# Token mixing with two shifted projections: a load that is issued later, and a crossbar transpose in two parts

## The chip, the cores and the metric

The kernel runs on one core of a Trainium2 chip. A core has TensorE (PE in the profile) for matmuls, VectorE (DVE), ScalarE (ACT) and GpSimd (POOL) for elementwise work, and SyncE (SP), which here only issues transfers. Sixteen DMA engines move data between the chip's memory and the core's SBUF. Each engine takes its instructions in program order; across engines the order is set by semaphores. The metric is the device time of the whole kernel in microseconds.

## The reference, cut to what matters

```python
batch, seq_len, d_model = (16, 2048, 256)
x_prev[:, 1:, :] = x[:, :-1, :]                       # the row before; zeros for the first
xv = x * time_mix_v + x_prev * (1 - time_mix_v)
xr = x * time_mix_r + x_prev * (1 - time_mix_r)
v = xv @ value_weight
r = xr @ receptance_weight
out = (sigmoid(r) * v) @ output_weight
# xk and k are computed in the reference too, and nothing uses them
```

The output is fp32, 16 x 2048 x 256. The kernel folds `time_mix` into the weights, so that what it has to form per element is `x + c * x_prev` with `c = 1/time_mix - 1`, once for r and once for v.

## The kernel before: the parts that the change touches

The 32768 rows are worked off in 64 units of 512 rows, four to a batch. For unit g, TensorE computes r(g) and v(g) into PSUM (psum_r, psum_v, one buffer each), ScalarE takes the sigmoid of r(g), VectorE multiplies it with v(g) into z(g), TensorE multiplies z with the output weight into psum_o (one buffer), and ScalarE evicts psum_o into o_sb, from which SyncE stores.

The matmuls need x with channels on the partitions. For batches 0 to 10 TensorE transposes blocks of 128x128 and ScalarE copies them to `xt`; for the last five batches the crossbar of the DMA does it, by transposes that SyncE issues. Batches 0 and 1 are loaded by units, and batch 2 onward by whole batches. Within a batch `xt` has 16 slots of 128 rows, and one slot 0 ahead of them: as rows are dealt to partitions, `x_prev` of slot j is slot j - 1, and slot 0 is slot 16 moved by one row. That copy is made by ScalarE for the last five batches.

```python
    def load(b):                                  # GpSimd issues: fp32 in memory, bf16 in SBUF
        if b not in x_bf:
            x_bf[b] = xpool.tile([P, J, D], BF16, name="x_bf")
        if b < BYUNIT:                            # batches 0 and 1: four loads, one for each unit
            for e in range(UB):
                nc.gpsimd.dma_start(...)          # cut
            return
        if b < B - 1:
            run = 8192 if b < LONG else 16384
            return nc.gpsimd.dma_start(out=x_bf[b], in_=rows(b), max_dma_last_dim=run)
        return [...]                              # the last batch in two halves (cut)
    ...
    for e in (2, 3):
        nc.gpsimd.dma_start(out=x_first[:, e - 2], in_=unit_rows(x, 0, e)[:, 0])
    nc.gpsimd.dma_start(out=wo_bf, in_=output_weight.rearrange("(ko p) n -> p ko n", p=P))
    load(1)
    load(2)
    ...
    def by_dma(b, lo, hi, after=None):            # slots lo to hi of batch b through the crossbar
        op = nc.sync.dma_start_transpose(
            out=xt[b][:, 1 + lo : 1 + hi].rearrange("p j k c -> p (j k) c"),
            in_=x_bf[b][:, lo:hi].rearrange("p j d -> p (j d)"),
        )
        if after is not None:                     # not beside a load
            tc.add_manual_dep(op.ins, after.ins.name, SYNC, reason="not beside a load")
```

`x + c * x_prev` is built in two steps: a scaled copy of the shifted slots (`mix = c * xt`, by VectorE in L263, by GpSimd in L273, by ScalarE in L520), and an add of the unshifted slots by VectorE (L285). The loop over the units, cut to what matters here:

```python
    for g in range(NU - 1):
        ...                                       # r(g) on TensorE, sigmoid on ScalarE
        advance(...)                              # TensorE transposes for later units
        for b in range(B - 5, B):
            if g == max(UB * (b - 2) - 1, CROSS + (b > B - 5)):
                new_xt(b)
                if b == B - 5:                    # batch 11
                    for pair in kept.pop(g):
                        store(nc.sync, *pair, after=half_load)
                    by_dma(b, 0, J, last_load)
                else:
                    by_dma(b, 0, J)
                ...
            if g == UB * (b - 1) + 1:             # slot 0 out of the last slot (L554)
                nc.scalar.copy(out=xt[b][:, 0, :, 1:P], in_=xt[b][:, J, :, 0 : P - 1])
        if LATE_O < g < NU - 2:
            output(g - 2, z_prev2)                # TensorE: o(g-2); ScalarE: eviction (L351)
        ...
        if g == 1:
            scale_act(pieces(2)[1], (1,))
        ...                                       # scaled copies and adds on VectorE, v(g), z(g)
        for p in pooled[g]:
            wrap_slots(p, after=last)
            scale_pool(p, last)                   # GpSimd: the scaled copy L273
        for p in held[g]:
            add(p)
        ...
        if g == 1:
            advance(4)
```

Of the kernel before, what the change touches and what calls it, by code (L numbers as in the profile page):

```python
# [15 lines left out]
def kernel(  # L16
# [30 lines left out]
    J = S // P  # L47
    UJ = 4
# [47 lines left out]
    def rows(b):  # L96
        return x[b].rearrange("(p j) d -> p j d", p=P)

    def unit_rows(t, b, e, n=1):

        return t[b, e * TU : (e + n) * TU, :].rearrange("(e p j) d -> p e j d", p=P, j=UJ)

    def load(b):
        if b not in x_bf:
            x_bf[b] = xpool.tile([P, J, D], BF16, name="x_bf")
        if b < BYUNIT:
            for e in range(UB):
                nc.gpsimd.dma_start(
                    out=x_bf[b][:, e * UJ : (e + 1) * UJ, :], in_=unit_rows(x, b, e)[:, 0]
# [5 lines that stand above are left out]
        return [  # L115
            nc.gpsimd.dma_start(out=x_bf[b][:, j : j + J // 2], in_=rows(b)[:, j : j + J // 2])
            for j in (0, J // 2)
        ]
# [30 lines left out]
        nc.gpsimd.dma_start(out=x_first[:, e - 2], in_=unit_rows(x, 0, e)[:, 0])  # L149
    nc.gpsimd.dma_start(out=wo_bf, in_=output_weight.rearrange("(ko p) n -> p ko n", p=P))  # L150
    load(1)
    load(2)

    def warm_up(n):
        ps = ps_t_pool.tile([P, P], FP32, name="ps_t")
# [34 lines left out]
    def by_dma(b, lo, hi, after=None):  # L190
# [5 lines that stand above are left out]
        if after is not None:  # L196
            tc.add_manual_dep(op.ins, after.ins.name, SYNC, reason="not beside a load")
# [51 lines left out]
    def slots(piece, off=0):  # L249

        b, _, lo, hi = piece
        j = lo // P + (lo // TU if b < BYUNIT else 0) + off
        return slice(j, j + (hi - lo) // P)

    def mixed(piece):
        b, m, lo, hi = piece
        j = lo // P % (2 * UJ)
        return mix[(b * S + lo) // (2 * TU)][:, m, j : j + (hi - lo) // P]
# [42 lines left out]
    def project_unmixed(ps, mo):  # L301


        parts = [(w_prev[:, ko], ko, 0) for ko in range(KO)]
        parts += [(w_bf[:, 0, ko], ko, 1) for ko in range(KO)]
        for n, (w, ko, lo) in enumerate(parts):
            nc.tensor.matmul(
                out=ps[:, mo, :],
                lhsT=w[:, mo * P : (mo + 1) * P],
                rhs=xt[0][:, lo : lo + UJ, ko],  # L310
                start=(n == 0),
                stop=(n == len(parts) - 1),
            )
# [92 lines left out]
    def tile_for(b):  # L406

        if b not in mix:
            mix[b] = mixpool.tile([P, 2, 2 * UJ, KO, P], BF16, name="mix")

    def pieces(g):

        b, e = divmod(g, UB)
        tile_for(g // 2)
        return [(b, m, e * TU, (e + 1) * TU) for m in range(2)]

    def wrap_slots(piece, one=None, after=None):


        b, _, lo, _ = piece  # L420
        by_unit = b < BYUNIT
        key = (b, lo // TU if by_unit else UB - 1)
        if key not in late_copies:
            return
        kos = slice(0, KO) if one is None else slice(one, one + 1)
        if one in (None, KO - 1):
            late_copies.remove(key)
        j = slots(piece).start if by_unit else 0
        n = UJ if by_unit else J
        if by_unit and j > 0:  # L430
            engine = nc.vector if key == (0, 1) else nc.gpsimd
            engine.tensor_copy(out=xt[b][:, j, kos, 0:1], in_=xt[b][:, j - 1, kos, P - 1 : P])
        op = (nc.vector if after is None else nc.gpsimd).tensor_copy(  # L433
            out=xt[b][:, j, kos, 1:P], in_=xt[b][:, j + n, kos, 0 : P - 1]
        )
        if after is not None:
            tc.add_manual_dep(op.ins, after.ins.name, SYNC, reason="one at a time")
# [4 lines left out]
    def advance(limit):  # L442
        nonlocal tnext, half_load, last_load
        while tnext <= min(limit, NU - 1):
            b, e = divmod(tnext, UB)
            if b == 1 and e > 0:
                load(b + e + 1)
            elif b > 1 and e == 0 and b + 5 < B:
                if b == 2:
                    load(6)  # L450
                last_load = load(b + 5)
                if b + 5 == B - 1:
                    half_load, last_load = last_load
            if tnext < NU - BYDMA:
                transposes(tnext)
            tnext += 1
# [60 lines left out]
    def scale_act(piece, kos):  # L517
        b, m, _, _ = piece
        for ko in kos:
            nc.scalar.activation(  # L520
                out=mixed(piece)[:, :, ko],
                in_=xt[b][:, slots(piece), ko],
                func=ACT.Copy,
                scale=c_sb[:, m, ko : ko + 1],
            )

    z_prev2 = z_prev = None
    for g in range(NU - 1):
        ps_r = ps_r_pool.tile([P, KO, TU], FP32, name="psum_r")
        if g == 0:  # L530
            project_unmixed(ps_r, 0)
            advance(1)
            project_unmixed(ps_r, 1)
            wrap_slots(pieces(1)[0])
            scale(pieces(1)[0])
            last = add(pieces(1)[0])
        else:
            project(ps_r, g, 0)
        s_sb = zpool.tile([P, KO, TU], BF16, name="s_sb")
        nc.scalar.activation(out=s_sb, in_=ps_r, func=ACT.Sigmoid)  # L540
        advance(START_T[g] if g < len(START_T) else g + LOOK - (g == CROSS - 1))
# [3 lines that stand above are left out]
                if b == B - 5:  # L545
                    for pair in kept.pop(g):
                        store(nc.sync, *pair, after=half_load)
                    by_dma(b, 0, J, last_load)
                else:
                    by_dma(b, 0, J)  # L550
                for pair in kept.pop(g, []):
                    store(nc.sync, *pair)
            if g == UB * (b - 1) + 1:
                nc.scalar.copy(out=xt[b][:, 0, :, 1:P], in_=xt[b][:, J, :, 0 : P - 1])  # L554
        if LATE_O < g < NU - 2:
            output(g - 2, z_prev2)
        for p in products.get(g + 1, []):
            if g >= FREE and p[0][1] == 1:
                scale_act(p[0], (0,))
        for p in [q for q, _ in products[g]] + pooled[g]:  # L560
            last_unit_of = p[3] // TU - 1
            need = last_unit_of if p[0] < BYUNIT else min(last_unit_of + 1, UB - 1)
            assert UB * p[0] + need < tnext, (g, p, tnext)
            if g > AHEAD or p not in pooled[g]:
                wrap_slots(p)
        if g == 1:
            scale_act(pieces(2)[1], (1,))
        for p, kos in products[g]:
            if not (g - 1 >= FREE and p[1] == 1):
                scale(p, kos)  # L570
        for p in sums[g]:
            last = add(p)
        for p in pooled[g]:
            if p[0] >= BYUNIT:
                wrap_slots(p)
        ps_v = ps_v_pool.tile([P, KO, TU], FP32, name="psum_v")
        project(ps_v, g, 1)
        if g == 0:
            scale_act(pieces(1)[1], (0,))
            advance(2)  # L580
        z_sb = zpool.tile([P, KO, TU], BF16, name="z_sb")
        n = TU // 2 if g == NU - 2 else TU
        for c in range(0, TU, n):
            nc.vector.tensor_tensor(  # L584
                out=z_sb[:, :, c : c + n],
                in0=s_sb[:, :, c : c + n],
                in1=ps_v[:, :, c : c + n],
                op=ALU.mult,
            )
        for p in pooled[g]:  # L590
            wrap_slots(p, after=last)
            scale_pool(p, last)
        for p in held[g]:
            add(p)
        if z_prev is not None and not LATE_O <= g < NU - 3:
            output(g - 1, z_prev)
        if g == AHEAD - 2:
            scale_act(pieces(AHEAD)[0], (1,))
        if g == 1:
            advance(4)  # L600
        z_prev2, z_prev = z_prev, z_sb
# [31 lines left out]
```

## Time and profile before

The time before is 202.42 us, the median of three runs (202.08 to 202.89). The profiled execution spans 201.2 us.

| Part of the profile | What it says |
|---|---|
| idle time of TensorE | 201.2 - 195.1 = 6.1 us |
| TensorE, one matmul group of r, v or o | 0.86 to 0.87 us from one to the next |
| VectorE z (L584), 128x1024 | 1200 ns |
| VectorE add (L285), 128x1024 | 707 ns on average |
| GpSimd product (L273), 128x1024 | 1112 ns on average |
| ScalarE eviction (L351) | 1023 ns |
| mean use of the chip's memory | 337 GB/s over the span |
| crossbar transposes, issue to landing | 7.3 to 12.6 us |

The profile gives, for each group of instructions, the source line, the engine, what is written from what, and the idle time of the engine just ahead of it with the work that ended it. "PEld" is TensorE's loading of weights, which lies beside its matmuls. "SPq" and "POOLq" are the issuing queues of SyncE and GpSimd; the window of an issue is not the time of the transfer. A wait for several things is put down to the one that came last. The line numbers are those of the kernel before; in the changed kernel those between the removed line and the loop are one lower.

### The profile page before, as it was taken

The page shows a single profiled execution, that of the slowest core. Times are in us where ns is not written, and L with a number is a line of the kernel's source. Part 1 is how long each engine was busy: PE and PEld are TensorE (multiplying, and loading weights), DVE is VectorE, ACT ScalarE, POOL GpSimd, SP SyncE. Part 2 cuts the span into 40 slices and gives each one's busy share as a digit, 9 for nine tenths or more (in the row PEclk, how much of TensorE's full clock was granted, in tenths as well). Part 3 has the DMA queues.
Part 4 walks back from the last instruction along what each step waited for, and adds up shares of the span by engine and source line. Part 5 has one row for each costly group of instructions (what it writes and reads, how often), then busy time and mean ns, then how long its engine had stood idle before and what let it go on. Part 6 is the DMA issues. An engine that isn't in the chain of part 4 may idle for free.

```text
span 201.2 us, 3884 instructions
## 1 busy us (share of the span) xinstructions
PE 195.1 (97%) x1419; PEld 125.3 (62%) x1419; DVE 186.1 (93%) x292; ACT 181.0 (90%) x204; POOL 84.1 (42%) x115
## 2 busy tenths in 40 slices
PE   8989999999999999999999999998999999999992
PEld 6656676666666666666666666654656566555671
DVE  0899999999999999999999999999999999999982
ACT  3699899999999999999999999898999999999982
POOL 1766562452542543434452543443344444444200
PEclk9999999999999999999999999999999999999999
DMA  5899999999999999999999999899999999999675
GB/s 171 216 170 216 220 279 274 278 280 275 291 312 299 285 275 287 290 279 283 292 277 301 309 397 302 288 192 205 289 255 407 352 207 262 412 419 408 257 311 210
DMA packets 32410, 57.00 MB, mean 283 GB/s; under 512 B 21764, under 2 KB 23048, under 8 KB 28424
## 3 DMA queue, kind: packets, MB, share of 16 engines
q1 hardware_dynamic: 28176, 40.24, 58.8%
q0 software_dynamic: 4064, 16.39, 40.5%
q8 instruction: 11, 0.18, 0.3%
q10 hardware_dynamic: 152, 0.13, 0.2%
q14 instruction: 7, 0.06, 0.1%
HBM read 34.34 MB, written 33.55 MB: 337 GB/s over the span
## 4 chain that ended last, share of the span: by engine, by line
PE 80%; DMA 9%; DVE 4%; issue 2%; POOL 1%; ACT 1%; SPq 0%; DVEq 0%
PE psum_v L293 24%; PE psum_o L317 23%; PE psum_r L293 23%; PE ps_t L211 8%; DMA xt<-x_bf 4%; DMA x_bf<-in_x_dram 3%; DMA w_f<-n_receptance_weight_dram 2%; DVE mix L285 2%; DVE z_sb L584 2%; PE ps_t L317 1%; DVE mix L263 1%; POOL x_first L149 1%; ACT o_sb L351 1%; PE ps_t L293 0%; SPq L130 0%
## 5 line engine op out<-in xcount | busy, mean ns | idle before, releaser
L273 POOL TENSOR_SCALAR mix<-xt,c_sb 128x1024 bf16<-128x1024 bf16 (+1 forms) x55 | 61.2, 1112 | 93.6 <-DVE mix L285 84.3
L285 DVE TENSOR_TENSOR mix<-mix,xt 128x1024 bf16<-128x1024 bf16 x112 | 78.1, 707 | 1.9 <-DVE mix L263 0.5
L584 DVE TENSOR_TENSOR z_sb<-s_sb,psum_v 128x1024 bf16<-128x1024 bf16 (+1 forms) x64 | 76.7, 1200 | 3.3 <-PE psum_v L293 1.8
L293 PEld LDWEIGHTS <-w_bf 128*128 128x128 bf16 x516 | 48.7, 98 | 38.5 <-DVE mix L285 0.7
L540 ACT ACTIVATE s_sb<-psum_r 128x1024 bf16<-128x1024 f32 x63 | 65.3, 1036 | 3.3 <-PE psum_r L293 2.7
L351 ACT COPY o_sb<-psum_o 128x1024 f32<-128x1024 f32 x60 | 61.4, 1023 | 7.1 <-PE psum_o L317 7.0
L293 PE MATMUL psum_v<-mix,w_bf 128*128 128x512 bf16 (+1 forms) x256 | 65.3, 377 | 0.5 <-DVE mix L285 0.3
L293 PE MATMUL psum_r<-mix,w_bf 128*128 128x512 bf16 (+1 forms) x252 | 64.2, 377 | 0.1
L317 PE MATMUL psum_o<-wo_bf,z_sb 128*128 128x256 bf16 x486 | 63.2, 272 | 0.8 <-ACT o_sb L351 0.8
L317 PEld LDWEIGHTS <-z_sb 128*128 128x128 bf16 x512 | 49.8, 98 | 21.3 <-issue 2.2
L228 ACT COPY xt<-ps_t 128x1024 bf16<-128x1024 bf16 x36 | 37.0, 1041 | 0.0
L211 PEld LDWEIGHTS <-x_bf 128*128 128x128 bf16 x320 | 20.9, 98 | 8.9 <-DMA x_bf<-in_x_dram 0.7
L211 PE MATMUL ps_t<-ident,x_bf 128*128 128x128 bf16 x320 | 23.9, 219 | 0.2 <-DMA x_bf<-in_x_dram 0.2
L263 DVE TENSOR_SCALAR mix<-xt,c_sb 128x1024 bf16<-128x1024 bf16 (+1 forms) x49 | 22.0, 458 | 0.0
L520 ACT ACTIVATE mix<-xt,c_sb 128x1024 bf16<-128x1024 bf16 x12 | 13.9, 1157 | 0.0
L285 DVE TENSOR_TENSOR mix<-mix,xt_first 128x1024 bf16<-128x1024 bf16 x15 | 10.5, 709 | 0.3 <-ACT xt_first L228 0.3
L114 POOL DMA_DIRECT2D x_bf<-in_x_dram x13 | 8.6, 659 | 0.0
L263 DVE TENSOR_SCALAR mix<-xt_first,c_sb 128x512 bf16<-128x512 bf16 x21 | 6.2, 347 | 0.4 <-ACT xt_first L221 0.3
L228 ACT COPY xt_first<-ps_t 128x1024 bf16<-128x1024 bf16 x6 | 6.1, 1019 | 0.0
L157 PE MATMUL ps_t<-zeros 128*128 128x128 bf16 x30 | 3.6, 313 | 1.0 <-DVE zeros L90 1.0
L273 POOL TENSOR_SCALAR mix<-xt_first,c_sb 128x512 bf16<-128x512 bf16 x6 | 4.2, 694 | 0.5
L433 POOL COPY xt_first<-xt_first 128x254 bf16<-128x254 bf16 x5 | 2.0, 395 | 5.4 <-DVE mix L285 3.6
(70 smaller groups left out, 52.0 us busy)
## 6 DMA issues: line engine op xcount, KB each, us to landing
out_dram<-o_sb SPq DMA_DIRECT2D x28, 1024.0 KB, 14.9
x_bf<-in_x_dram POOLq DMA_DIRECT2D x13, 1024.0 KB, 24.8
out_dram<-o_sb SPq DMA_DIRECT2D x4, 512.0 KB, 2.8
out_dram<-o_sb SPq DMA_DIRECT2D x6, 256.0 KB, 2.5
o_sb<-in_x_dram SPq DMA_DIRECT2D x4, 256.0 KB, 4.0
x_bf<-in_x_dram POOLq DMA_DIRECT2D x4, 256.0 KB, 7.5
x_bf<-in_x_dram POOLq DMA_DIRECT2D x2, 512.0 KB, 11.5
x_first<-in_x_dram POOLq DMA_DIRECT2D x2, 256.0 KB, 4.1
```

Source lines behind the costliest of these rows:

```text
L114: return nc.gpsimd.dma_start(out=x_bf[b], in_=rows(b), max_dma_last_dim=run)
L211: nc.tensor.transpose(out=ps[:, jj], in_=src[:, jj, ko * P : (ko + 1) * P], identity=idn)
L228: nc.scalar.copy(out=xt[b][:, j0 : j0 + UJ], in_=ps)
L263: nc.vector.tensor_scalar(out=mixed(piece)[:, :, ko], in0=xt[b][:, slots(piece), ko], scalar1=c_sb[:, m, ko : ko + 1], scalar2=None, op0=A ...
L273: op = nc.gpsimd.tensor_scalar(out=mixed(piece)[:, :, 1], in0=xt[b][:, slots(piece), 1], scalar1=c_sb[:, m, 1:2], scalar2=1.0, op0=ALU.mul ...
L285: return nc.vector.tensor_tensor(out=mixed(piece), in0=mixed(piece), in1=xt[b][:, slots(piece, 1)], op=ALU.add)
L293: nc.tensor.matmul(out=ps[:, mo, :], lhsT=w_bf[:, m, ko, mo * P : (mo + 1) * P], rhs=mixed((b, m, e * TU + lo, e * TU + hi))[:, :, ko], st ...
L317: nc.tensor.matmul(out=ps[:, slot, :], lhsT=z[:, ko, jj * P : (jj + 1) * P], rhs=wo_bf[:, ko, :], start=(ko == 0), stop=(ko == KO - 1),)
L351: nc.scalar.copy(out=o_sb[b][:, j0 : j0 + UJ, :], in_=ps)
L520: nc.scalar.activation(out=mixed(piece)[:, :, ko], in_=xt[b][:, slots(piece), ko], func=ACT.Copy, scale=c_sb[:, m, ko : ko + 1],)
L540: nc.scalar.activation(out=s_sb, in_=ps_r, func=ACT.Sigmoid)
L584: nc.vector.tensor_tensor(out=z_sb[:, :, c : c + n], in0=s_sb[:, :, c : c + n], in1=ps_v[:, :, c : c + n], op=ALU.mult,)
```

## The change

Two things are moved, and the computation stays what it was.

```diff
     nc.gpsimd.dma_start(out=wo_bf, in_=output_weight.rearrange("(ko p) n -> p ko n", p=P))
     load(1)
-    load(2)
@@ in the loop over the units
                 if b == B - 5:
                     for pair in kept.pop(g):
                         store(nc.sync, *pair, after=half_load)
-                    by_dma(b, 0, J, last_load)
+                    by_dma(b, J - UJ, J, last_load)
+                    by_dma(b, 0, J - UJ, last_load)
                 else:
                     by_dma(b, 0, J)
@@
         if g == 1:
+            load(2)
             scale_act(pieces(2)[1], (1,))
```

The load of batch 2 was the last of the transfers that GpSimd issues before it does any elementwise work. It is now issued after GpSimd's first product (and a copy of two columns behind it), so that this product need not wait for the issue. On GpSimd's own list of instructions nothing else changes its place.

The transpose of batch 11, the first one by the crossbar, was one instruction over 16 slots (32 blocks of 128x128). It becomes two: first the last four slots (8 blocks), then the other twelve (24 blocks). ScalarE's copy of the last slot into slot 0 (L554) now waits only for the first of the two; the scaled copies of the batch's first half wait for the second.

## The prediction

> **What bounds the kernel now.** I read the page first, then the table of waits, then the chain of waits in order of time, then the timeline around the two places that the diff touches (10 to 17 us and 129 to 146 us). All times below are us from the span's start; z, r, v and o stand for the product of gate and value on VectorE and for TensorE's matmuls into psum_r, psum_v and psum_o, with the number of the unit in brackets.
>
> The page says TensorE is busy nearly all the time, and VectorE and ScalarE are close behind:
>
> ```profile
> PE 195.1 (97%) x1419; PEld 125.3 (62%) x1419; DVE 186.1 (93%) x292; ACT 181.0 (90%) x204; POOL 84.1 (42%) x115
> ```
>
> So at most about 6 us of 201.2 can be had from waits of TensorE. The table of waits (engine, line, releaser: us in total, times, longest us) has these that the change could touch:
>
> ```profile
> PE psum_o L317 <- ACT o_sb L351: 0.8, 1, 0.8
> ...
> ACT xt L554 <- DMA xt<-x_bf: 0.7, 1, 0.7
> PEld L211 <- DMA x_bf<-in_x_dram: 0.7, 2, 0.4
> ...
> PE psum_v L293 <- DVE mix L285: 0.3, 1, 0.3
> ```
>
> The first two rows are one event. The timeline at 129 to 139 us (start, us, engine, line, what; idle before it in brackets) shows it:
>
> ```profile
> 129.66 10.55 SPq L192 DMA_TRANSPOSE xt<-x_bf  x2
> ...
> 137.03 0.40 ACT L554 COPY xt<-xt 128x254 bf16<-128x254 bf16 x1 [0.71 <-DMA xt<-x_bf]
> ...
> 137.34 1.01 ACT L351 COPY o_sb<-psum_o 128x1024 f32<-128x1024 f32 x1
> 137.52 1.12 POOL L273 TENSOR_SCALAR mix<-xt,c_sb 128x1024 bf16<-128x1024 bf16 x1 [2.08 <-ACT xt L554]
> 138.02 1.17 DVE L285 TENSOR_TENSOR mix<-mix,xt 128x1024 bf16<-128x1024 bf16 x1
> ...
> 138.39 1.03 PE L317 MATMUL psum_o<-wo_bf,z_sb 128*128 128x256 bf16 x8 [0.76 <-ACT o_sb L351]
> ```
>
> The chain of waits runs through the same rows: the transpose for 7.35 from 129.66, the copy, the eviction, o(40). Batch 11's crossbar transpose is issued at 129.66 and lands 7.35 later, at 137.0. ScalarE is ready for the copy of the last slot (L554) when its sigmoid ends, at 135.30 + 1.02 = 136.32, and then sits idle for 0.71. Behind it, in program order, waits the eviction of psum_o, which has one buffer, and so o(40) on TensorE starts at 138.39 where r(42) let go of TensorE at 136.61 + 0.87 = 137.48: TensorE loses 0.91.
>
> Near the start, the rows that matter are:
>
> ```profile
> 10.53 0.73 POOL L114 DMA_DIRECT2D x_bf<-in_x_dram  x1
> ...
> 11.26 0.73 POOL L273 TENSOR_SCALAR mix<-xt_first,c_sb 128x512 bf16<-128x512 bf16 x1
> ...
> 12.03 0.69 DVE L285 TENSOR_TENSOR mix<-mix,xt_first 128x1024 bf16<-128x1024 bf16 x1 [0.27 <-ACT xt_first L228]
> ...
> 12.78 1.04 PE L293 MATMUL psum_v<-mix,w_bf 128*128 128x512 bf16 x4 [0.35 <-DVE mix L285]
> ...
> 14.84 0.62 PE L211 MATMUL ps_t<-ident,x_bf 128*128 128x128 bf16 x8 [0.16 <-DMA x_bf<-in_x_dram]
> ```
>
> GpSimd's issue of batch 2's load (10.53, 0.73) stands ahead of its first product (11.26 to 11.99); VectorE's add at 12.03 needs that product (the page names ScalarE's L228, which ended at 12.01, but the add reads nothing of it); v(1) waits 0.35 for the add. Two rows further on, GpSimd's second product runs at 15.06 (0.69) and VectorE's next add at 15.49 (0.80).
>
> **What the Trainium skill says.** *SBUF — State Buffer*, section "Who interferes with whom": a VectorE instruction with two SBUF inputs and a GpSimd instruction that reads SBUF contend for one shared port, and the later one fully blocks. The trace agrees: the add at 15.49 overlaps the product that ends at 15.75 and takes 0.80 instead of 0.68; the add at 138.02 overlaps the product that ends at 138.64 and takes 1.17. Both end about 0.54 after the product does. *DMA: Bandwidth & Descriptors*, section "Queues, rings and completion order": within a ring descriptors are consumed in order. The trace agrees, in the table of DMA issues asked for one issue at a time: batch 1's four quarters, issued from 8.38 on, land at 14.78 (issue plus 6.4) up to 19.2, and batch 2's load, issued at 10.53, lands 13.3 later at 23.8. *Perfetto Trace Analysis*, section "Per-instruction lifecycle: what the profiler-reported window actually captures": the window of a DMA issued by SyncE is descriptor generation, and the landing comes later. Here the first transpose's window is 5.43 and the landing 7.35 - 5.43 = 1.92 after its end. No page has a time for splitting a transpose.
>
> **The change, part 1: batch 2's load behind the first product.** No work is added or removed; one issue of 0.73 moves.
> - The product can start when the four quarter issues (8.38 + 2.18 = 10.56) and the add it is made to follow (9.93 + 0.69 = 10.62) are over: about 10.66 instead of 11.26, end 11.39.
> - VectorE is held by z(0) until 10.54 + 1.21 = 11.75, so the add moves from 12.03 to 11.76: 0.27 gained. v(1) moves from 12.78 to 12.45, o(0) from 13.65 to 13.32.
> - Then TensorE meets the transposes of batch 1's first unit, which need the quarter that lands at 14.78. That quarter was issued before batch 2's load in both kernels, in the same queue, so I leave its landing. The wait of 0.16 at 14.84 grows to 0.5 and the whole gain of TensorE is gone.
> - VectorE's gain goes too: z(1) ends at 15.30 instead of 15.57, but GpSimd's second product stays at 15.06 to 15.75 (it hangs on ScalarE's L520, 13.71 + 0.75 = 14.46, which does not move), so the next add ends at 15.75 + 0.54 = 16.29 as before.
> - Batch 2 is first read by TensorE at 25.5, landing 23.8. Its issue comes some 1 us later (about 11.5), but the queue holds batch 1 until 19.2, so no gap arises.
>
> Sum of part 1: 0, at most 0.1 to 0.2 if the quarter lands earlier because GpSimd writes no further descriptors meanwhile.
>
> **Part 2: batch 11's transpose in two, last slots first.** One instruction of 32 blocks of 128x128 becomes one of 8 and one of 24; the copy L554 waits only for the 8, and all other readers of batch 11's first half wait for the 24.
> - Landing of the 8: 129.66 + 5.43 x 8/32 + 1.92 = 132.9, over 3 us before ScalarE wants it.
> - Landing of the 24: the two are issued in turn. Between the transposes of batches 11 and 12 the gap was 135.27 - (129.66 + 5.43) = 0.18. So 129.66 + 5.43 + 0.18 + 1.92 = 137.19, 0.18 later than now.
> - ScalarE: L554 from 136.33 to 136.74, eviction to 137.76, o(40) at 137.80 instead of 138.39: 0.59 gained on TensorE, with 0.3 of wait left.
> - VectorE must follow, since z(42) is what v(43) waits for. The product of batch 11 needs the 24: start 137.19 + 0.09 (the lag seen between 137.43 and 137.52) = 137.28, end 138.40, so the blocked add ends at 138.95 instead of 139.19. z(42) then comes at 139.94 by VectorE (140.18 - 0.24) and at 139.81 by TensorE, against 140.40. z(43) comes by TensorE at 142.41, by VectorE at 142.37, against 143.00: the full 0.59.
> - After that both engines run a fixed pattern. z starts at 145.74, 151.01, 156.28 and 161.55, every 5.27 for two units, where TensorE alone would need 5.20, so VectorE sets the pace there; moved 0.59 earlier it stays so up to the end. Batch 12's transpose shifts by 0.18; nothing waited for it (its copy ran at 147.56 without a wait).
>
> Sum of part 2: -0.59. **Both: 202.42 - 0.59 - 0 = 201.8; I say 201.9,** for the rivals below mostly lie on the slow side.
>
> **The rivals.**
> - *The second transpose costs more than the gap.* If a transpose has a fixed cost of d beyond 0.18 that lands the 24 later, GpSimd's product moves with it and blocks VectorE's add longer. VectorE's gain at z(43) is 0.82 - (0.18 + d), so up to d = 0.05 nothing is lost, d = 0.4 leaves 0.24 and d = 0.65 leaves none. For it: windows of transposes of one size range from 4.90 to 10.7. Against: those were the ones beside heavy stores. It would make 202.2 to 202.5.
> - *VectorE is the bound, and a gain of TensorE is given back.* For it: the pace of 5.27 against 5.20. Against: its own idle, 0.22 and 0.17 before z(42) and z(43), plus 0.24 of blocking, is given up in the same place. If it holds in part, 202.1.
> - *Part 1 is not swallowed.* If the first quarter lands 0.3 earlier, everything after may move up to 0.2 to 0.3: 201.6.
> - *Part 1 hurts.* Batch 2's descriptors are now written while VectorE adds; if batch 2 landed after 25.5, TensorE would wait. There is 1.7 of room. Unlikely; 203.
>
> **Range and chances.** The three runs before spread over 0.81 (202.08 to 202.89), and the mechanisms span from 0 to 0.9 gained. So 201.3 to 202.5 should hold it 8 times in 10. Two per cent are 4.05 us; no wait in reach has that size: faster 0.01, within 0.98, slower 0.01.
>
> **What would show each step.** In the profile of the changed kernel: no wait of the copy L554 for a DMA; TensorE's wait for the eviction near 138 down from 0.76 to about 0.2; GpSimd's product released by the transpose near 137.2; the add after it well under 1.17. At the start: GpSimd's first product near 10.7, VectorE's gap of 0.27 and TensorE's 0.35 gone, and TensorE's wait for batch 1's first quarter up from 0.16 to about 0.5, with the psum_r matmuls after it still near 15.3. I am wrong if those matmuls come earlier (part 1 carries), or if the 24 land later than 137.6 (the split costs), or if the last load lands at another time and moves the 129.66 with it.

## The result, and the profile after

The changed kernel took 201.55 us (median of 6 runs, 201.44 to 201.71). The kernel before took 202.65 us (6 runs, 202.08 to 203.65) beside it. The ratio is 0.9942 [0.9914, 0.9969]. Two later comparisons of the same two kernels, with more runs, gave less: 0.9985 [0.9974, 0.9997] and 0.9988 [0.9974, 1.0002], with medians of 201.91 and 201.84. So the predicted 201.9 is where the changed kernel is; the 1.1 us between the two medians of the first comparison is more than the change brings in the larger ones. The profiled span fell from 201.2 to 199.8.

The page of the changed kernel, its busy shares and the shares of the chain of work that ended last:

```profile
PE 194.9 (98%) x1419; PEld 125.1 (63%) x1419; DVE 185.6 (93%) x292; ACT 180.7 (90%) x204; POOL 83.6 (42%) x115
...
PE 89%; DVE 5%; issue 2%; ACT 2%; POOL 0%; DVEq 0%; POOLq 0%
```

TensorE does the same 195 us of work. In the chain of before, 9% were steps of DMA; here there is none, and TensorE carries 89%. That difference is not the change's alone: a second trace of the kernel before, read below, has no step of DMA in its chain either (TensorE 86%), and a second trace of the changed kernel has 5%. The timeline near the start (start, us, engine, line, what; idle before it in brackets; L272, L284, L292, L210, L316, L350 and L585 are the product, the add, r and v, the transposes, o, the eviction and z):

```profile
10.54 0.69 POOL L272 TENSOR_SCALAR mix<-xt_first,c_sb 128x512 bf16<-128x512 bf16 x1 [0.26 <-DVE mix L284]
...
11.31 0.77 POOL L114 DMA_DIRECT2D x_bf<-in_x_dram  x1
...
11.39 0.68 DVE L284 TENSOR_TENSOR mix<-mix,xt_first 128x1024 bf16<-128x1024 bf16 x1
...
12.13 1.04 PE L292 MATMUL psum_v<-mix,w_bf 128*128 128x512 bf16 x4 [0.17 <-DVE mix L284]
...
14.08 0.45 PEld L210 LDWEIGHTS <-x_bf 128*128 128x128 bf16 x8 [0.32 <-DMA x_bf<-in_x_dram]
...
14.08 0.62 PE L210 MATMUL ps_t<-ident,x_bf 128*128 128x128 bf16 x8
...
14.42 0.68 POOL L272 TENSOR_SCALAR mix<-xt_first,c_sb 128x512 bf16<-128x512 bf16 x1
...
129.24 10.32 SPq L191 DMA_TRANSPOSE xt<-x_bf  x3
...
135.57 0.40 ACT L554 COPY xt<-xt 128x254 bf16<-128x254 bf16 x1
135.86 1.02 ACT L350 COPY o_sb<-psum_o 128x1024 f32<-128x1024 f32 x1
...
136.70 1.12 POOL L272 TENSOR_SCALAR mix<-xt,c_sb 128x1024 bf16<-128x1024 bf16 x1 [1.89 <-DMA xt<-x_bf]
136.94 1.03 PE L316 MATMUL psum_o<-wo_bf,z_sb 128*128 128x256 bf16 x8
...
137.38 0.97 DVE L284 TENSOR_TENSOR mix<-mix,xt 128x1024 bf16<-128x1024 bf16 x1
...
139.28 1.21 DVE L585 TENSOR_TENSOR z_sb<-s_sb,psum_v 128x1024 bf16<-128x1024 bf16 x1
```

At the start, the product now runs ahead of the load's issue, the add follows it, v(1) is at 12.13 (it was at 12.78), and the transposes of batch 1 are at 14.08 (14.84). They still wait a little for batch 1's first quarter: their weight load shows 0.32, and they begin 1.07 after o(0) at 13.01, where 0.87 is the distance without a wait, so TensorE loses 0.20 (in before 14.84 - 13.65 - 0.87 = 0.32). Near batch 11, where the row of three transposes holds the two parts and batch 12's, the copy L554 runs at 135.57 with no bracket: it waits for nothing. The eviction behind it and o(40) at 136.94 (138.39) follow without a gap. The only thing that still waits for the transposes is GpSimd's product. The table of waits (engine, line, releaser: us in total, times, longest us) has neither L554 nor the wait of o for the eviction any more; of the rows shown of before these answer:

```profile
POOL mix L272 <- DMA xt<-x_bf: 1.9, 1, 1.9
...
PEld L210 <- DMA x_bf<-in_x_dram: 0.6, 2, 0.3
```

Where the 1.4 us of span went, read as shifts against the trace of before:

| Point | before | after | shift |
|---|---|---|---|
| v(0) on TensorE | 9.27 | 8.99 | -0.28 |
| first transposes of batch 1 | 14.84 | 14.08 | -0.76 |
| v of the unit near 33 us | 33.19 | 32.55 | -0.64 |
| o(40) | 138.39 | 136.94 | -1.45 |
| z(42) | 140.40 | 139.28 | -1.12 |
| z(44) | 145.74 | 144.44 | -1.30 |
| span | 201.2 | 199.8 | -1.4 |

Three terms can be told apart. First, -0.28 is there before either part of the change can act: GpSimd's cast of the receptance weight, which waits for a load that SyncE issues as before, ran at 5.49 instead of 5.91. Second, 0.64 - 0.28 = 0.36 arises between v(0) and 33 us, where only part 1 acts. Third, 1.4 - 0.64 = some 0.8 arises at batch 11. Whether these belong to the change or to the run is what the experiments had to tell.

### The profile page after: what moved, and what is told of

Read it like the earlier page. It is cut to its first block, busy times and chain, and to the rows that moved or that the text cites. A ratio compares the mean times of both kernels' runs of the same rounds, so it can differ in the third digit from the quotient of the medians.

```text
span 199.8 us, 3885 instructions
## 1 busy us (share of the span) xinstructions
PE 194.9 (98%) x1419; PEld 125.1 (63%) x1419; DVE 185.6 (93%) x292; ACT 180.7 (90%) x204; POOL 83.6 (42%) x115
## 4 chain that ended last, share of the span: by engine, by line
PE 89%; DVE 5%; issue 2%; ACT 2%; POOL 0%; DVEq 0%; POOLq 0%
PE psum_v L292 26%; PE psum_o L316 25%; PE psum_r L292 24%; PE ps_t L210 8%; DVE mix L284 2%; PE ps_t L156 2%; DVE z_sb L585 1%; PE ps_t L316 1%; DVE mix L262 1%; ACT s_sb L539 1%; ACT xt_first L220 1%; PE psum_r L234 1%; ACT mix L519 1%; PE psum_r L306 1%; ACT xt L227 1%
## 5 line engine op out<-in xcount | busy, mean ns | idle before, releaser
L272 POOL TENSOR_SCALAR mix<-xt,c_sb 128x1024 bf16<-128x1024 bf16 (+1 forms) x55 | 61.0, 1109 | 93.1 <-DVE mix L284 81.7
L284 DVE TENSOR_TENSOR mix<-mix,xt 128x1024 bf16<-128x1024 bf16 x112 | 77.9, 705 | 1.9 <-DVE mix L262 0.5
L585 DVE TENSOR_TENSOR z_sb<-s_sb,psum_v 128x1024 bf16<-128x1024 bf16 (+1 forms) x64 | 76.6, 1199 | 2.9 <-PE psum_v L292 1.4
L292 PEld LDWEIGHTS <-w_bf 128*128 128x128 bf16 x516 | 48.7, 98 | 38.5 <-issue 0.6
L350 ACT COPY o_sb<-psum_o 128x1024 f32<-128x1024 f32 x60 | 61.4, 1024 | 6.7 <-PE psum_o L316 6.7
L292 PE MATMUL psum_v<-mix,w_bf 128*128 128x512 bf16 (+1 forms) x256 | 65.3, 377 | 0.3 <-DVE mix L284 0.2
L292 PE MATMUL psum_r<-mix,w_bf 128*128 128x512 bf16 (+1 forms) x252 | 64.3, 377 | 0.1
L316 PE MATMUL psum_o<-wo_bf,z_sb 128*128 128x256 bf16 x486 | 63.2, 272 | 0.0
L316 PEld LDWEIGHTS <-z_sb 128*128 128x128 bf16 x512 | 49.8, 98 | 20.4 <-issue 1.4
L210 PEld LDWEIGHTS <-x_bf 128*128 128x128 bf16 x320 | 20.9, 98 | 8.8 <-DMA x_bf<-in_x_dram 0.6
L210 PE MATMUL ps_t<-ident,x_bf 128*128 128x128 bf16 x320 | 23.9, 219 | 0.0
L284 DVE TENSOR_TENSOR mix<-mix,xt_first 128x1024 bf16<-128x1024 bf16 x15 | 10.6, 713 | 0.1
L272 POOL TENSOR_SCALAR mix<-xt_first,c_sb 128x512 bf16<-128x512 bf16 x6 | 4.1, 684 | 0.8 <-DVE mix L284 0.3
```

Of the source, the lines that this page charges most:

```text
L210: nc.tensor.transpose(out=ps[:, jj], in_=src[:, jj, ko * P : (ko + 1) * P], identity=idn)
L272: op = nc.gpsimd.tensor_scalar(out=mixed(piece)[:, :, 1], in0=xt[b][:, slots(piece), 1], scalar1=c_sb[:, m, 1:2], scalar2=1.0, op0=ALU.mul ...
L284: return nc.vector.tensor_tensor(out=mixed(piece), in0=mixed(piece), in1=xt[b][:, slots(piece, 1)], op=ALU.add)
L292: nc.tensor.matmul(out=ps[:, mo, :], lhsT=w_bf[:, m, ko, mo * P : (mo + 1) * P], rhs=mixed((b, m, e * TU + lo, e * TU + hi))[:, :, ko], st ...
L316: nc.tensor.matmul(out=ps[:, slot, :], lhsT=z[:, ko, jj * P : (jj + 1) * P], rhs=wo_bf[:, ko, :], start=(ko == 0), stop=(ko == KO - 1),)
L350: nc.scalar.copy(out=o_sb[b][:, j0 : j0 + UJ, :], in_=ps)
```

## The experiments

The line numbers of the kernels below are moved by what is added or taken out above them; the names of the tiles tell which instruction a row is. The theory after the first comparison: part 1 gains some 0.3 by letting GpSimd's first product go earlier, and part 2 gains only when the last load, and with it batch 11's transposes, comes late, as in the trace of before. The rivals: part 1 gains nothing and the shift is the chance of an early weight; part 1 gains through the queue of loads, not through the product; part 2 gains in every run; the gain of part 2 comes from splitting, whatever the order.

### The two kernels again, and each part alone

`before_again` and `after_again` are the two kernels unchanged. The other two undo one part each:

```diff
 # p1_only: the changed kernel, with part 2 undone
-                    by_dma(b, J - UJ, J, last_load)
-                    by_dma(b, 0, J - UJ, last_load)
+                    by_dma(b, 0, J, last_load)
 # p2_only: the changed kernel, with part 1 undone
     load(1)
+    load(2)
 ...
-            load(2)
```

> The kernel before, unchanged, for a second trace and for the spread. In its first trace the receptance weight landed at 5.85 and batch 1's first quarter at 14.78; in the changed kernel's trace they landed at 5.45 and 14.03. If the weight's landing is chance (my theory: 0.3 to 0.4 of the early 0.64 is no effect of the change), this trace shows a landing of the weight anywhere from 5.4 to 5.9, and everything up to 14 us moves with it. If the changed kernel itself brings it earlier, the weight lands again at 5.8 or later. Ratio to the kernel before 1.000 within 0.003; the wait of the copy L554 is there again, between 0.3 and 1.2 us.

> Only batch 2's load moved; batch 11's transpose in one instruction. Theory of the prediction (the gain is swallowed by the landing of batch 1's first quarter): ratio 0.999 to 1.001, v(1) 0.3 earlier, the transposes of batch 1's first unit not earlier against the weight's landing, a wait of about 0.4 ahead of them. Rival (part 1 carries): 0.3 to 0.6 us faster, ratio 0.997 to 0.9985, and the quarter lands about 8.6 after the weight instead of 8.9. In both the copy L554 waits about 0.7 or more and TensorE loses some 0.9 there.

> Only batch 11's transpose in two; batch 2's load where it was. Theory: 0.6 to 0.7 us faster, ratio 0.9965 to 0.997, the copy L554 without a wait, o(40) no more than 0.35 after r(42) is through, the 24 blocks landing 7.3 to 7.6 after the issue. If the difference between the two kernels lies mainly at the start, then under 0.3 us faster, ratio above 0.9985.

> Both parts, unchanged, beside the others on the same chip. If the parts add, its gain is that of the two alone together: with the theory of the prediction 0.6 to 0.7 us (ratio 0.9965 to 0.997), with the rival 1.0 to 1.2 us (ratio 0.994 to 0.995). The landing of the weight tells whether the early 0.64 comes again: if it is chance, TensorE's first matmul on batch 1 lies 8.6 to 8.9 after the weight in both kernels.

Measured against 75 runs of before (median 202.17), 22 runs each:

| Kernel | median us | ratio | profiled span |
|---|---|---|---|
| before_again | 202.22 | 1.0 [0.9984, 1.0016] | 200.3 |
| p1_only | 201.97 | 0.9997 [0.9981, 1.0013] | 200.2 |
| p2_only | 202.00 | 0.9992 [0.9981, 1.0003] | 200.2 |
| after_again | 201.91 | 0.9985 [0.9974, 0.9997] | 199.8 |

Neither part alone can be told from zero by these ratios, and p2_only is far from the 0.6 to 0.7 us expected of it; both together are just past zero. The surprise is in the trace of before_again, a second trace of the very kernel that the prediction was read from. Its timeline:

```profile
128.42 10.33 SPq L192 DMA_TRANSPOSE xt<-x_bf  x2
...
136.11 0.40 ACT L554 COPY xt<-xt 128x254 bf16<-128x254 bf16 x1
...
137.48 1.03 PE L317 MATMUL psum_o<-wo_bf,z_sb 128*128 128x256 bf16 x8
```

With one transpose instruction of 32 blocks, the copy waits for nothing and o(40) is at 137.48, not at 138.39. The transposes were issued at 128.42, where the trace of before had 129.66: the last load, which they wait for, was down 1.24 earlier. Of the 0.91 between the two o(40), 0.10 was there before, at o(39) (134.87 and 134.77): so 0.8 of the gain seen at o(40) was the lateness of one run. In p1_only, too, they were issued at 128.44 and the copy waited for nothing. In the eight traces in which the transposes wait for the last load (filler4 below, whose whole course is later, left out) the issue lies at 128.13 to 128.44 in five, and at 129.04, 129.24 and 129.66 in after_again, after and before. In before_again the landing is 7.1 after the issue, 0.6 ahead of the copy; so an estimate from this trace is that the copy would have waited there only for an issue after some 129.0.

### Batch 11's transposes made late on purpose

To see part 2 without this chance, three kernels (all with part 1) tie the transposes to z(38) instead of the last load. That is a wait for VectorE at a fixed place; they were issued at 130.19, 130.05 and 130.32. The three differ only in the split and its order. As the tie also holds SyncE's queue, they are to be compared with one another, and not with before:

```diff
-                    by_dma(b, J - UJ, J, last_load)
-                    by_dma(b, 0, J - UJ, last_load)
 ...
-            nc.vector.tensor_tensor(
+            z_op = nc.vector.tensor_tensor(
 ...
+        if g == CROSS:
+            by_dma(B - 5, 0, J, z_op)         # late_one
+            # late_two:      by_dma(B - 5, J - UJ, J, z_op); by_dma(B - 5, 0, J - UJ, z_op)
+            # late_reversed: by_dma(B - 5, 0, J - UJ, z_op); by_dma(B - 5, J - UJ, J, z_op)
```

> The changed kernel with batch 11's transpose in one instruction again, and tied to the end of z(38) instead of to the last load. That fixes its issue at about 129.7 in the changed kernel's time, as late as in the first trace of before, whatever the load does. Theory: landing 7.3 to 7.5 later, at about 137.1; the copy L554 waits 1.2 to 1.5; o(40) starts 1.5 or more after r(42) is through; about 1.0 to 1.4 us slower than the changed kernel, so some 1 us slower than before (ratio 1.004 to 1.006), in all runs and not in some. Rival (the waits of batch 11 don't reach the end): ratio below 1.001.

> The same tie to z(38), with the transpose in two, last slots first. Theory: the copy L554 doesn't wait; the 24 blocks land at about 137.2 and GpSimd's product with them; VectorE's add behind it is blocked by 0.4 to 0.6; 0.6 to 1.0 us faster than the same tie with one instruction (ratio to before 1.000 to 1.002). Rival (VectorE is the bound and gives the gain back): under 0.3 faster than with one instruction.

> The same tie, in two instructions, first slots first: the split without the order. Theory: the copy waits for the second instruction, which lands 0 to 0.2 after the undivided one; 0 to 0.3 slower than with one instruction. If the second instruction has a fixed cost of its own of 1 us or more, 0.7 to 1.2 slower. If the gain came from splitting alone (shorter instructions beside the stores), as fast as with the last slots first.

Measured, against 19 runs of before (median 202.13):

| Kernel | median us (runs) | ratio | span |
|---|---|---|---|
| late_one | 202.97 (5) | 1.0037 [1.0025, 1.0049] | 201.2 |
| late_two | 202.32 (13) | 1.0013 [1.0002, 1.0024] | 200.5 |
| late_reversed | 203.41 (6) | 1.0067 [1.0043, 1.0091] | 201.6 |

The timeline of late_one at batch 11 brings back what the trace of before had:

```profile
130.19 9.95 SPq L191 DMA_TRANSPOSE xt<-x_bf  x2
...
137.07 0.40 ACT L552 COPY xt<-xt 128x254 bf16<-128x254 bf16 x1 [0.86 <-DMA xt<-x_bf]
...
137.90 1.32 DVE L284 TENSOR_TENSOR mix<-mix,xt 128x1024 bf16<-128x1024 bf16 x1
...
138.44 1.03 PE L316 MATMUL psum_o<-wo_bf,z_sb 128*128 128x256 bf16 x8 [0.92 <-ACT o_sb L350]
...
143.04 1.22 DVE L583 TENSOR_TENSOR z_sb<-s_sb,psum_v 128x1024 bf16<-128x1024 bf16 x1 [0.18 <-PE psum_v L292]
```

The same rows in the timeline of late_two, with v(43) added:

```profile
130.05 10.22 SPq L191 DMA_TRANSPOSE xt<-x_bf  x3
...
135.96 0.41 ACT L552 COPY xt<-xt 128x254 bf16<-128x254 bf16 x1
...
137.33 1.03 PE L316 MATMUL psum_o<-wo_bf,z_sb 128*128 128x256 bf16 x8
...
137.45 1.12 POOL L272 TENSOR_SCALAR mix<-xt,c_sb 128x1024 bf16<-128x1024 bf16 x1 [2.26 <-PE psum_r L292]
137.77 1.34 DVE L284 TENSOR_TENSOR mix<-mix,xt 128x1024 bf16<-128x1024 bf16 x1
...
141.29 1.02 PE L292 MATMUL psum_v<-mix,w_bf 128*128 128x512 bf16 x4 [0.21 <-DVE z_sb L583]
...
142.42 1.22 DVE L583 TENSOR_TENSOR z_sb<-s_sb,psum_v 128x1024 bf16<-128x1024 bf16 x1
```

The split takes the copy's wait away. o(40) comes 138.44 - 137.33 = 1.11 earlier, of which 0.14 was there before (o(39) at 134.76 and 134.62): 0.97 gained. z(43) gains only 143.04 - 142.42 - 0.14 = 0.48, since VectorE's blocked add ends at 139.11, hardly before late_one's 139.22, and TensorE now waits 0.21 for VectorE at v(43). The medians differ by 0.65, the means by 0.53. Half of what TensorE gained is given back to VectorE.

The order alone makes the difference. The timeline of late_reversed, in two with the wrong part first:

```profile
130.32 10.17 SPq L191 DMA_TRANSPOSE xt<-x_bf  x3
...
137.55 0.40 ACT L552 COPY xt<-xt 128x254 bf16<-128x254 bf16 x1 [1.20 <-DMA xt<-x_bf]
...
138.91 1.03 PE L316 MATMUL psum_o<-wo_bf,z_sb 128*128 128x256 bf16 x8 [1.25 <-ACT o_sb L350]
```

The copy waits longer than with one instruction: from the first issue to the copy 137.55 - 130.32 = 7.23, against 137.07 - 130.19 = 6.88. The split itself costs some 0.35, and with its order reversed this shows in full (median 0.44 above late_one). These costs are each read from one trace.

### What part 1 works through

Two kernels put a memset on GpSimd in the place from which the load was taken away, one about as long as the load's issue and one four times 128x1024:

```diff
     load(1)
+    filler = consts.tile([P, 748], BF16)      # filler4: [P, 2 * TU], and four memsets
+    nc.gpsimd.memset(filler, 0.0)
```

> The changed kernel with four memsets of 128x1024 on GpSimd ahead of its first product, which add no transfers: the product is held back by the sum of their times (some 1.5 to 2.5 us), later than the load's issue held it, while the queue of loads is that of the changed kernel. Theory now (the product is on the path, and the first quarter's landing swallows only what it is late by in a run): v(1) and all after it 1 us or more later, the kernel 0.8 to 1.8 us slower than the changed one, ratio to before 1.003 to 1.008. Theory of the prediction (the landing and GpSimd's second product swallow it): about 0.5 of the delay is swallowed in every run. If the path never led through the product: ratio 0.998 to 0.999, as the changed kernel.

> The changed kernel with one memset of 128x748 on GpSimd ahead of the first product: about 0.73 us at the 1.0 us that one of 128x1024 took, as long as the issue of batch 2's load, while the load stays issued late. It tells whether part 1 works through the product (theory now: v(1) again 3.5 to 3.7 after v(0), the first matmul on batch 1 again 5.4 to 5.6 after v(0), 0.25 to 0.4 slower than the changed kernel) or through the queue of loads, or not at all (v(1) late, but the first matmul on batch 1 at 5.0 to 5.2 after v(0); no slower than the changed kernel within 0.1).

> The changed kernel once more, as the yardstick for the three beside it. So far it took 201.93 in the mean beside 202.24 of before on one chip, and 201.56 beside 202.74 on another. Theory now: part 1 gives about 0.35 in every run (the first matmul on batch 1 came 5.5 after v(0) in the three traces with the load in its old place and 5.1 in the six with it moved), part 2 gives nothing when the last load lands by 128.6 and up to 0.7 when it lands near 129.7. So 0.3 to 0.6 faster than before, ratio 0.997 to 0.9985.

filler4 took 206.0 us (6 runs, ratio 1.0178 [1.0146, 1.0211]): its memsets took 4.00 us, about twice what was guessed, and the time was 3.9 above the 202.13 of before, not the 0.8 to 1.8 above the changed kernel that was expected. Its timeline:

```profile
11.16 4.00 POOL L154 MEMSET filler<- 128x1024 bf16 x4
...
15.87 0.69 DVE L287 TENSOR_TENSOR mix<-mix,xt_first 128x1024 bf16<-128x1024 bf16 x1 [2.96 <-POOL mix L275]
...
16.62 1.04 PE L295 MATMUL psum_v<-mix,w_bf 128*128 128x512 bf16 x4 [3.30 <-DVE mix L287]
...
17.49 1.84 PE L319 MATMUL psum_o<-wo_bf,z_sb 128*128 128x256 bf16 x8
```

So GpSimd's first product is on the path: what stands ahead of it moves VectorE's add and v(1), which comes 16.62 - 9.62 = 7.00 after v(0), and the end. How much of the 3.9 is the delay itself can't be read here, since TensorE also ran at half its clock for some 3 us behind the idle time (last section). filler073, whose load is as late as in the changed kernel, took 202.10 (14 runs, 0.9992 [0.9974, 1.0009]) and after_third, the changed kernel once more, 201.84 (22 runs, 0.9988 [0.9974, 1.0002]), both beside 55 runs of before (median 202.27). These times can't be told apart; the traces can. The timeline of filler073:

```profile
10.65 0.75 POOL L153 MEMSET filler<- 128x748 bf16 x1
...
11.36 0.71 POOL L274 TENSOR_SCALAR mix<-xt_first,c_sb 128x512 bf16<-128x512 bf16 x1
...
12.10 0.69 DVE L286 TENSOR_TENSOR mix<-mix,xt_first 128x1024 bf16<-128x1024 bf16 x1
12.13 0.77 POOL L114 DMA_DIRECT2D x_bf<-in_x_dram  x1
...
14.60 0.61 PE L212 MATMUL ps_t<-ident,x_bf 128*128 128x128 bf16 x8
```

The load is behind the product, the product is no earlier than with the load in its old place (2.28 after v(0), where before had 1.99 and p2_only 2.25), and batch 1's transposes start 14.60 - 9.08 = 5.52 after v(0). To leave out most of the chance of the weight, all traces but filler4's are measured from v(0) on TensorE, in us:

| Traces | v(1) | transposes of batch 1 | v near 33 us |
|---|---|---|---|
| load in the old place: before, before_again, p2_only | 3.62 (3.51 to 3.77) | 5.47 (5.33 to 5.57) | 24.02 (23.92 to 24.17) |
| filler073: load late, product late | 3.77 | 5.52 | 24.21 |
| load late, product early: the other nine | 3.35 (3.14 to 3.49) | 5.18 (4.96 to 5.50) | 23.73 (23.56 to 23.87) |

The nine are after, after_again, after_third, p1_only, the three late ones, and the two of the next section. The mean gains are 0.27, 0.30 and 0.29: what v(1) gains is still there 20 us later, and at 33 us no trace of one kind reaches the other, though the nearest two lie only 0.05 apart (23.87 and 23.92). In the one trace with the small filler it is gone. So the traces say that part 1 works through the product and not through the queue of loads; the times of unprofiled runs are too spread to show it.

Not everything that the product gains arrives. In after_again the chain of waits (start, us, what) runs so:

```profile
7.11 4.84 DMA x_first<-in_x_dram
...
11.99 0.62 PE ps_t L210 x8
12.61 0.86 PE psum_v L292 x4
13.47 0.87 PE psum_o L316 x8
14.35 0.45 PE ps_t L210 x8
```

Here the transposes of the last unit of batch 0, which wait for its load (issued at 7.11, in TensorE's use at 11.99), hold v(1), and not the add; five of the nine traces show that wait (0.18 to 0.27 long). A transfer has taken the place of the wait removed.

### Batch 11's transposes earlier

If lateness is what costs, an earlier issue should gain. eight_ahead lets the 8 blocks go when the first half of the last load is down, no_gate lets both parts go then, beside the other half:

```diff
-                    by_dma(b, J - UJ, J, last_load)
-                    by_dma(b, 0, J - UJ, last_load)
+                    by_dma(b, J - UJ, J, half_load)
+                    by_dma(b, 0, J - UJ, last_load)   # no_gate: half_load here too
```

> The changed kernel with the 8 blocks of the last slots tied to the first half of the last load (landed near 124.5) and only the 24 tied to the second half. Theory: the 8 are issued near 127 to 128, when slot 0 is cleared; the 24 are issued when the load lands and land some 5.5 to 6.0 after that instead of 7.3, so GpSimd's product no longer waits for them; 0 to 0.3 faster than the changed kernel, the more the later the load lands. Rival: the 8 blocks beside the load delay its landing by as much as they save; no difference.

> Both parts of batch 11's transpose tied to the first half of the last load only, so that they run beside its second half. Theory: issued near 127.0 to 127.6, landed by 135.5 even beside the load, no wait of ScalarE, GpSimd or TensorE on batch 11: 0 to 0.3 faster than the changed kernel. Rival (a transpose beside a load is slow, which the gate is there for): the 24 land later than 137.2, and it is slower by 0.2 or more.

eight_ahead took 201.77 (22 runs, 0.9975 [0.996, 0.999]) and no_gate 201.85 (9 runs, 0.9982 [0.9967, 0.9997]), beside after_third's 201.84. Neither is shown to be better than the changed kernel. In eight_ahead the 8 were issued at 125.15 and the 24 at 128.99, and yet GpSimd's product waited until 136.98 for the 24, 7.99 from issue to use where 5.5 to 6.0 had been expected. The timeline of no_gate shows that the earlier issue bought nothing:

```profile
14.67 0.51 PE L210 MATMUL ps_t<-ident,x_bf 128*128 128x128 bf16 x6 [0.19 <-DMA x_bf<-in_x_dram]
...
125.08 14.78 SPq L191 DMA_TRANSPOSE xt<-x_bf  x3
...
136.99 1.12 POOL L272 TENSOR_SCALAR mix<-xt,c_sb 128x1024 bf16<-128x1024 bf16 x1 [1.73 <-DMA xt<-x_bf]
```

The transposes were issued 4.2 earlier than in after (129.24), and GpSimd's product still waited for them until 136.99 (136.70 in after). From issue to use they took 11.9, against 136.70 - 129.24 = 7.46 behind the load. The packets of the queues say more. In no_gate the queue of the loads is empty from just past 128, and SyncE's queue, on which a store of 1 MB issued at 124.57 stands ahead of the transposes, still moves large packets between 128 and 129 (0.43 MB in 61 packets). Small packets set in between 129 and 130 (234 packets, then 961 in the next 2 us), hardly earlier than in after (28, then 1091), and from 130 to 134 fewer of them pass than in after (1446 against 2770). So what was issued 4.2 earlier mostly stood in the queue, and the long time is no measure of a transpose beside a load; what makes the packets few after 130 is open. The first row matters below: here batch 1's first quarter landed at 14.65, and TensorE did wait for it.

## Why the prediction was right, and which term was off

**Total.** 201.9 was said; the three medians of the changed kernel are 201.55, 201.91 and 201.84. The number is right, in part by luck: a gain of 0.5 from 202.42 was forecast, while the larger comparisons give 0.24 to 0.30 (from the ratios 0.9988 and 0.9985) from medians of before of 202.17 to 202.27. The sum behind it, 0 and -0.59, is not what those runs show.

**Part 1, said to be 0: mis-sized, some -0.3 in the traces.** The step up to v(1) held: 0.33 was said, 0.27 was found. What failed is the step "I leave its landing. The wait of 0.16 at 14.84 grows to 0.5 and the whole gain of TensorE is gone." The quarter of batch 1 was taken to land at 14.78 whatever the change does. Its landing belongs to the run: over the traces of all these kernels it took 5.5 to 6.4 from its issue, and the first trace of before had the longest. In the changed kernel's first trace it landed at 14.03, and only 0.20 of TensorE's time was lost to it. The swallowing is real where the quarter is late against v(0): in no_gate it landed at 14.65 and TensorE waited 0.19, and the distance from v(0) was 5.50, no gain there. The second reason given, that GpSimd's second product stays at 15.06, failed too: it ran at 14.42, and the copy ahead of it waited for VectorE's add, which had moved. The rival "part 1 is not swallowed" is what happened, and the sign of being wrong that was named with it is there: r behind those transposes came at 14.54, not near 15.3. How much of the 0.3 reaches the end of an unprofiled run isn't settled: p1_only's ratio is 0.9997 [0.9981, 1.0013], so from 0.4 gained to 0.3 lost.

**Part 2, said to be -0.59: mechanism right, and about right in size where it applies.** The copy no longer waits, o(40) follows, and the difference between late_two and late_one is 0.65 in the medians and 0.53 in the means, where the copy's wait was 0.86 instead of 0.71. The landing of the 24 blocks was said to be 7.53 after the issue; the product began 7.46 after it. The rival "VectorE is the bound, and a gain of TensorE is given back" holds in part: 0.97 at o(40) became 0.48 at z(43). But the wait that the term removes was read from one trace whose last load came late. In the two other traces with one instruction behind the last load, before_again and p1_only, the transposes were issued 1.2 earlier, and it wasn't there. The step that failed is to price a wait of one trace as if each run had it; the prediction's last sign of being wrong, that the last load lands at another time, is what came. So over many runs part 2 is worth less: p2_only's ratio is 0.9992 [0.9981, 1.0003], 0.16 gained and not told from zero.

**The split's own cost,** named as a rival: 0.35 at the last landing in late_reversed. It doesn't hurt in the right order, as the part that is wanted first goes first and the product can take the rest late.

**Batch 2's load.** It was said to have 1.7 of room; no wait of TensorE for it appeared in the changed kernel.

**VectorE's blocked add.** The rule of *SBUF — State Buffer*, section "Who interferes with whom", which the prediction used, holds in the changed kernel: the add at 137.38 overlaps the product that ends at 137.82 and takes 0.97, where the free add takes 0.68. It ends 0.53 after the product and not a whole 0.68, so not all of the add's time stands behind it; why isn't shown.

**Open.** Why the receptance weight is down at some 5.5 in one run and 6.5 in another, and what moves the landing of the last load by 1.5, wasn't found. The comparison of 6 runs gave some four times the gain of the larger ones; a share of late runs of before among its six would explain that, but unprofiled runs don't show where their time went, and as the comparisons were made on several chips, a difference between chips stays as possible.

## What to carry to other kernels

A wait for a DMA that one trace shows may belong to that run: take a second trace of the same kernel before giving the wait a price, and where the gain depends on lateness, fix the lateness in an experiment and compare there. An issue of a transfer on GpSimd costs up to its window, 0.73 here, to whatever stands behind it on GpSimd, so what feeds the critical engine goes first. When a transfer is split, the part that is wanted first goes first; in the other order the split only costs.

## What was not expected of the hardware

- GpSimd's memset of 128x1024 bf16 took 1.00 us, nearly as long as its product of that shape (1.11).
- Behind 3.30 us of idle TensorE ran at half its clock for a while, and not at once: in filler4, v(1), the first group behind the idle time, still took 1.04. The granted clock in its trace is 1.00 up to 17.4, 0.50 from 17.6 to 20.8, and 1.00 again from 21.0. The eight matmuls of o at 17.49 took 1.84 instead of 1.04, and the r at 19.98 took 1.52 instead of 1.03. *TensorE: Matmul & The Clock Gate*, section "Part 1: The HAM clock gate (the "warmup" mystery)", says that the clock is halved after an idle window of some 3.4 us. The trace agrees on the half; the idle time here was 3.30.
- 32 blocks through the crossbar took 6.9 to 7.3 from issue to landing in one instruction (late_one, before_again, p1_only and before), 7.4 to 7.6 from issue to use in two (late_two, after and after_again; at most 7.4 in late_two, where the product may have waited for TensorE instead), and 11.9 in two when they were issued before the load's second half was down, with a store ahead of them in their queue (no_gate).
